# One product in two column parts, and one lower half ahead of an addition, in the feed forward of a hybrid block

## The chip, the cores and the metric

The kernel runs on one core of a Trainium2 chip. The time is the device time of one execution in microseconds (us), the median of several runs. Durations and waits come from one profiled execution, whose times count from the start of its span.

## The reference

The block works on 512 tokens of 1024 features in float32. It joins a convolution branch and a state space branch by gates, multiplies by an output matrix, adds the input, and then applies a gated feed forward of 2816 hidden columns. The change is in the last part:

```python
x = x + rms_norm(mixed, mix_post_g[i])
h = rms_norm(x, ffn_pre_g[i])
gt, up = jnp.split(h @ w_gate_up[i], 2, axis=-1)
f = (jax.nn.silu(gt) * up) @ w_down[i]
x = x + rms_norm(f, ffn_post_g[i])
```

## The kernel before

**Three matmuls for one.** Every large product is taken in a float32r format that TensorE reads. An operand is split in an upper half (a cast, on ScalarE) and a lower half (the value less the upper half, on VectorE, or on ScalarE with an adding DMA from POOL's queue). `mm3` (line 244) issues three matmuls: upper by upper (L246), upper weights by lower moving operand (L248, or L251 twice when it is cut), lower weights by upper moving operand (L252).

**The feed forward in units.** The first product of the feed forward, `h @ w_gate_up`, is made in 22 units `u` of 256 columns, even ones of the gate half and odd ones of the other. A unit is a two by two block product in seven block products of Strassen's kind instead of eight: a11, a12, s2, s1, s3, s4 and a22, by the blocks or sums of blocks of the moving operand (b11, b21, t2, t1, t3, b22, t4). Each has four steps `k` of three matmuls with 256 moving columns: 12 matmuls. `first(u)` issues a11 and a12, `x2` s2, `v1` s1, `x3` s3, `v2` s4, `x4` a22. They add up in PSUM banks that are called xy (parts `X` and `Y`), yv or v in the profile.

**What VectorE and ScalarE do for a unit.** They form the sums of weight blocks (`s1_u` to `s4_u`), the upper halves (`hi_s2_u` and so on, cast into whi_g, chi_g or dhi) and the lower halves (`lo_s2_u`, into wlo_g, clo_g or dlo). They also take results out of PSUM between the products: `begin(u)` copies `X` on ScalarE (`c{u}`) and adds `Y` to it on VectorE (`b{u}`, in line 1396), and only then may `x2` go on adding to the bank.

**Order.** VectorE and ScalarE work in lists written out by hand, `ORDER_DVE` and `ORDER_ACT`: each instruction named there is put behind the one named before it. TensorE's products follow each other in the order in which they are issued.

**Cuts.** `CUT_GU` lists (unit, product, step) for which `mm3` gets `cut=128`: the second of the three matmuls is then issued as two, columns 0 to 127 and 128 to 255 of the same operand and the same output. Two steps of the feed forward have it, and `CUT_PW` names two steps of the convolution's pointwise product in the same way.

Of the kernel before, what the change touches and what calls it, by code (L numbers as in the profile page):

```python
# [59 lines left out]
for _n, _c in PRM:  # L60
# [12 lines left out]
WARM = 7  # L73
CUT = 128
CUT_PW = ((1, "a12", 1), (0, "s3", 1))
CUT_GU = ((0, "a11", 1), (0, "s1", 2))
FIRST = {0: (0, 1), 1: (1, 2), 2: (2, 4), 4: (4, 6), 6: (6, NK)}
LOAD_AT = {0: 0, 1: 1, 2: 2, 3: 4, 5: 6}
RAW_AHEAD = 3
# [11 lines left out]
ADD_S1 = (3, 5)  # L91
ORDER_DVE = (
# [78 lines left out]
def block_kernel(ctx: ExitStack, tc: tile.TileContext, x, xT, x0, prm, hp, gp, wf, w, out):  # L171
# [72 lines left out]
    def mm3(ps, lh, ll, rh, rl, start, stop, more=False, cut=None):  # L244

        mark["pe"] = pe.matmul(ps, lh, rh, start=start, stop=False, skip_group_check=more)  # L246
        if cut is None:
            pe.matmul(ps, lh, rl, start=False, stop=False, skip_group_check=more)  # L248
        else:
            for c in (slice(0, cut), slice(cut, T // 2)):  # L250
                pe.matmul(ps[:, c], lh, rl[:, c], start=False, stop=False, skip_group_check=True)  # L251
        mark["pe3"] = pe.matmul(ps, ll, rh, start=False, stop=stop, skip_group_check=more)  # L252
        return mark["pe"]
# [996 lines left out]
    def product(ps, u, wn, mn, start):  # L1250
# [4 lines left out]
        for k in range(KB):  # L1255
            c = slice(k * P, (k + 1) * P)
            cut = CUT if (u, wn, k) in CUT_GU else None
            m = mm3(ps, wh[:, c], wl[:, c], mh[:, k], ml[:, k], start and k == 0, k == KB - 1, not start, cut)
# [544 lines left out]
```

## Time and profile before

| | us |
|---|---|
| median of 3 runs | 1023.25 (1023.2 to 1023.58) |
| the profiled execution | 1023.47 |
| its span | 1021.7 |
| TensorE, VectorE, ScalarE, GpSimdE busy | 1013.6, 847.3, 617.4, 106.6 |

The feed forward's first product begins at 689.2 us with unit 0 and ends at 908.3 with unit 21, where the down projection begins. A row of a timeline gives the start, the duration, the engine, the line, the operation, and output and inputs by name. The end of a matmul is modelled, so the starts are what to compare. `x2` behind a row means two such instructions in one row.

### The profile page before, as it was taken

How to read it: one execution, taken by the hardware profiler on the slowest of the kernel's cores; microseconds unless marked ns; L12 is line 12 of the kernel's file. 1: busy time of each engine (PE TensorE's matmuls, PEld its weight loads, DVE VectorE, ACT ScalarE, POOL GpSimd, SP SyncE). 2: the span in 40 equal slices, each digit the busy share in tenths (PEclk: the TensorE clock that was granted, in tenths of full speed). 3: DMA queues.
4: the chain of work that ended last, by engine and by line, in shares of the span. 5: the costliest groups of instructions: out<-in, count | busy, mean ns of one | idle time of the engine just before them, and what ended most of it. 6: DMA issues, size and time to landing. Idle time of an engine off the chain costs nothing.

```text
span 1021.7 us, 15941 instructions
## 1 busy us (share of the span) xinstructions
PE 1013.6 (99%) x6183; PEld 888.2 (87%) x6183; DVE 847.3 (83%) x1233; ACT 617.4 (60%) x1038; POOL 106.6 (10%) x138
## 2 busy tenths in 40 slices
PE   9999999999999999999999999999999999999997
PEld 7898889888888888888888899889999999998886
DVE  7899976959595879488987789679998887799974
ACT  7655775666656655663542776476665655568552
POOL 0101101110111012100110110011000000001001
PEclk9999999999999999999999999999999999999999
DMA  8567635645554456446252365635656355459622
GB/s 303 158 168 221 150 89 144 187 130 138 147 163 123 120 170 157 118 138 155 73 145 81 104 199 116 223 100 133 202 152 197 106 146 144 134 168 296 207 83 82
DMA packets 43803, 155.02 MB, mean 152 GB/s; under 512 B 5072, under 2 KB 6096, under 8 KB 42704
## 3 DMA queue, kind: packets, MB, share of 16 engines
q1 hardware_dynamic: 30672, 105.44, 30.2%
q0 software_dynamic: 11136, 43.00, 21.6%
q10 hardware_dynamic: 1920, 5.57, 1.6%
q8 instruction: 48, 0.79, 0.3%
q14 instruction: 27, 0.22, 0.1%
HBM read 149.73 MB, written 4.26 MB: 151 GB/s over the span
## 4 chain that ended last, share of the span: by engine, by line
PE 93%; DVE 3%; ACT 3%; issue 1%; POOL 0%; POOLq 0%; DVEq 0%; ACTq 0%
PE xy L252 4%; PE xy L246 4%; PE xy L248 4%; PE pso L246 3%; PE pso L248 3%; PE pso L252 3%; PE yv L252 3%; PE yv L246 2%; PE yv L248 2%; PE pz L252 2%; PE pz L248 2%; PE pz L246 2%; PE px L252 2%; PE px L246 2%; PE px L248 2%; PE pgs L252 1%
## 5 line engine op out<-in xcount | busy, mean ns | idle before, releaser
L514 DVE SCALAR_TENSOR_TENSOR a<-v,prm_t,a 128x511 f32<-128x511 f32 (+15 forms) x240 | 182.4, 763 | 15.3 <-ACT a L511 13.3
L202 ACT CAST whi<-raw 128x1024 fp32r<-128x1024 f32 x99 | 102.6, 1048 | 128.0 <-PE pso L248 36.6
L209 DVE TENSOR_TENSOR wlo<-raw,whi 128x1024 fp32r<-128x1024 f32 x58 | 70.6, 1219 | 33.0 <-ACT whi L202 32.8
L207 POOL DMA_DIRECT2D wlo<-in_w x41 | 36.5, 891 | 370.6 <-ACT wlo L206 165.0
L248 PE MATMUL pz<-wlo,hhi 128*128 128x512 f32 (+2 forms) x160 | 56.1, 351 | 0.2 <-DVE wlo L209 0.2
L252 PE MATMUL pz<-whi,hlo 128*128 128x512 f32 (+2 forms) x160 | 56.1, 352 | 0.0
L246 PE MATMUL pz<-whi,hhi 128*128 128x512 f32 (+2 forms) x160 | 55.4, 353 | 0.0
L246 PE MATMUL px<-hhi,whi 128*128 128x512 f32 x128 | 50.2, 392 | 0.0
L246 PE MATMUL pso<-yh,whi 128*128 128x512 f32 x128 | 50.2, 394 | 0.0
L252 PE MATMUL px<-hhi,wlo 128*128 128x512 f32 x128 | 49.8, 389 | 0.0
L248 PE MATMUL px<-hlo,whi 128*128 128x512 f32 x128 | 49.8, 389 | 0.0
L248 PE MATMUL pso<-yl,whi 128*128 128x512 f32 x128 | 49.8, 390 | 0.0
L252 PE MATMUL pso<-yh,wlo 128*128 128x512 f32 x128 | 49.7, 389 | 0.0
L1189 ACT CAST whi_g<-raw 128x1024 fp32r<-128x1024 f32 x40 | 41.2, 1051 | 10.6 <-PE yv L248 5.8
L601 DVE SCALAR_TENSOR_TENSOR x<-px,prm_t,x 128x511 f32<-128x511 f32 (+2 forms) x48 | 34.7, 742 | 13.8 <-ACT x L599 13.8
L1196 DVE TENSOR_TENSOR wlo_g<-raw,whi_g 128x1024 fp32r<-128x1024 f32 x34 | 41.3, 1220 | 4.0 <-ACT whi_g L1189 3.7
L206 ACT ACTIVATE wlo<-whi 128x1024 fp32r<-128x1024 f32 x41 | 43.3, 1056 | 0.3
L496 ACT ACTIVATE L<-L,nacs 128x128 f32<-128x128 f32 x128 | 38.8, 389 | 0.5 <-POOL L L489 0.4
L248 PEld LDWEIGHTS pz<-wlo,hhi 128*128 128x128 f32 x160 | 30.2, 188 | 4.5 <-DVE wlo L209 0.6
L246 PEld LDWEIGHTS pz<-whi,hhi 128*128 128x128 f32 x160 | 30.2, 189 | 3.9
L252 PEld LDWEIGHTS pz<-whi,hlo 128*128 128x128 f32 x160 | 30.1, 188 | 3.7
L1189 ACT CAST chi_g<-raw 128x1024 fp32r<-128x1024 f32 x24 | 24.9, 1051 | 7.9 <-PE yv L248 3.8
(761 smaller groups left out, 3459.6 us busy)
## 6 DMA issues: line engine op xcount, KB each, us to landing
raw<-in_w SPq DMA_DIRECT2D x182, 512.0 KB, 4.5
wlo<-in_w POOLq DMA_DIRECT2D x41, 512.0 KB, 6.7
L<-scr POOLq DMA_DIRECT2D x8, 1024.0 KB, 7.9
wlo_g<-in_w POOLq DMA_DIRECT2D x11, 512.0 KB, 7.4
clo_g<-in_w POOLq DMA_DIRECT2D x6, 512.0 KB, 5.5
pws<-in_w POOLq DMA_DIRECT2D x8, 256.0 KB, 5.8
pw_raws<-in_w SPq DMA_DIRECT2D x4, 512.0 KB, 6.3
xr<-in_x ACTq DMA_DIRECT2D x4, 512.0 KB, 4.1
```

The source lines that it names most:

```text
L202: mark[n, c.start] = act.copy(hi[:, c], src)
L206: act.activation(lo[:, c], hi[:, c].bitcast(F32), AF.Copy, scale=-1.0)
L207: mark["lo"] = pool.dma_start(lo[:, c], w[n][:, c].bitcast(F32R), accum_op=ALU.add)
L209: mark["wlo"] = dve.tensor_tensor(out=lo[:, c], in0=src, in1=hi[:, c].bitcast(F32), op=ALU.subtract)
L246: mark["pe"] = pe.matmul(ps, lh, rh, start=start, stop=False, skip_group_check=more)
L248: pe.matmul(ps, lh, rl, start=False, stop=False, skip_group_check=more)
L252: mark["pe3"] = pe.matmul(ps, ll, rh, start=False, stop=stop, skip_group_check=more)
L496: act.activation(L[:, h, c, :], L[:, h, c, :], AF.Exp, bias=nacs[:, c, HG * g + h : HG * g + h + 1])
L514: return dve.scalar_tensor_tensor(out=va[j][:, d:], in0=vs[j][:, : T - d], scalar=col("dw_w", j * KC + KC - 1 - d), in1=va[j][:, d:], op0= ...
L601: dve.scalar_tensor_tensor(out=a[:, d:], in0=ps[:, : T - d], scalar=col("ssm_w", i * KS + KS - 1 - d), in1=a[:, d:], op0=ALU.mult, op1=ALU ...
L1189: a_ = act.copy(hi, src)
L1196: d_ = dve.tensor_tensor(out=lo, in0=src, in1=hi.bitcast(F32), op=ALU.subtract)
```

## The change

The third step of the s2 product of unit 3 (step 2, counted from 0) is cut as well, and VectorE does `lo_s2_3` ahead of the addition `b3`.

```diff
-CUT_GU = ((0, "a11", 1), (0, "s1", 2))
+CUT_GU = ((0, "a11", 1), (0, "s1", 2), (3, "s2", 2))
...
-    "s3_3 x3_1 s2_3 s4_3 lo_s3_2 b3 lo_s2_3 lo_s1_3 x3_2 v2_1 lo_s3_3 g2_1 lo_a11_4 g3_1 g4_1 s1_4 s3_4 s2_4 v2_2 "
+    "s3_3 x3_1 s2_3 s4_3 lo_s3_2 lo_s2_3 b3 lo_s1_3 x3_2 v2_1 lo_s3_3 g2_1 lo_a11_4 g3_1 g4_1 s1_4 s3_4 s2_4 v2_2 "
```

On VectorE, around the addition b3 of unit 3 (xy_6491 is unit 3's bank; wlo_g_6536 is lo_s3_2, wlo_g_6626 is lo_s2_3 and dlo_6630 is lo_s1_3), before:

```order
867 L1196 TENSOR_TENSOR wlo_g_6536<-raw_6267,whi_g_6535 128x1024 [waits Activation_49]
868 L1396 TENSOR_TENSOR f_6544<-xy_6491,f_6544 128x256
869 L1196 TENSOR_TENSOR wlo_g_6626<-raw_6120,whi_g_6625 128x1024 [waits DMASW3_49,DMASW2_49,Activation_49]
870 L1196 TENSOR_TENSOR dlo_6630<-s_3_6619,dhi_6629 128x512
871 L1396 TENSOR_TENSOR sg_1_6698<-xy_6417,sg_1_6698 128x256 [waits PE_49,Activation_49]
```

and now:

```order
867 L1196 TENSOR_TENSOR wlo_g_6536<-raw_6267,whi_g_6535 128x1024 [waits Activation_49]
868 L1196 TENSOR_TENSOR wlo_g_6626<-raw_6120,whi_g_6625 128x1024 [waits DMASW3_49,DMASW2_49,Activation_49]
869 L1396 TENSOR_TENSOR f_6544<-xy_6491,f_6544 128x256
870 L1196 TENSOR_TENSOR dlo_6630<-s_3_6619,dhi_6629 128x512
871 L1396 TENSOR_TENSOR sg_1_6698<-xy_6417,sg_1_6698 128x256 [waits PE_49,Activation_49]
```

The addition and the lower half have changed places, and the rows behind them stand where they stood.

On TensorE, the s2 product of unit 3, before:

```order
3400 L246 MATMUL xy_6491<-t2h,whi_g_6625 128x256 [waits DVE_49,Activation_49]
3401 L248 MATMUL xy_6491<-t2l,whi_g_6625 128x256
3402 L252 MATMUL xy_6491<-t2h,wlo_g_6626 128x256 [waits DVE_49]
3403 L246 MATMUL xy_6491<-t2h,whi_g_6625 128x256
3404 L248 MATMUL xy_6491<-t2l,whi_g_6625 128x256
3405 L252 MATMUL xy_6491<-t2h,wlo_g_6626 128x256
3406 L246 MATMUL xy_6491<-t2h,whi_g_6625 128x256
3407 L248 MATMUL xy_6491<-t2l,whi_g_6625 128x256
3408 L252 MATMUL xy_6491<-t2h,wlo_g_6626 128x256
```

and now:

```order
3400 L246 MATMUL xy_6491<-t2h,whi_g_6625 128x256 [waits DVE_49,Activation_49]
3401 L248 MATMUL xy_6491<-t2l,whi_g_6625 128x256
3402 L252 MATMUL xy_6491<-t2h,wlo_g_6626 128x256
3403 L246 MATMUL xy_6491<-t2h,whi_g_6625 128x256
3404 L248 MATMUL xy_6491<-t2l,whi_g_6625 128x256
3405 L252 MATMUL xy_6491<-t2h,wlo_g_6626 128x256
3406 L246 MATMUL xy_6491<-t2h,whi_g_6625 128x256
3407 L251 MATMUL xy_6491<-t2l,whi_g_6625 128x128 x2
3408 L252 MATMUL xy_6491<-t2h,wlo_g_6626 128x256
```

Row 3407 is two matmuls of 128 columns instead of one of 256. The wait on VectorE in row 3402 is gone; the one in row 3400, on b3, now stands for the lower half too, since b3 comes behind it on VectorE.

## The prediction

> **What bounds the kernel now.** I read the page first, for the engine shares and the chain that ended last; then the busy time by stage; then, since TensorE turned out never to be idle, the start times of its matmuls in the timeline.
>
> ```profile
> PE 1013.6 (99%) x6183; PEld 888.2 (87%) x6183; DVE 847.3 (83%) x1233; ACT 617.4 (60%) x1038; POOL 106.6 (10%) x138
> PE 93%; DVE 3%; ACT 3%; issue 1%; POOL 0%; POOLq 0%; DVEq 0%; ACTq 0%
> ```
>
> TensorE is busy for 99% of the span and is 93% of the chain. So a change pays only if it makes TensorE's stream itself shorter. Busy time can't show that; the distance between the starts of two matmuls can. The changed place is at 720 us, in the first product of the feed forward, whose matmuls have 256 moving columns. Here is TensorE in two stretches (length, busy us, matmuls, granted clock, DMA share, GB/s):
>
> ```profile
> 703.77:718.73 14.96, 14.96 (x135) 1.00 0.53 141
> 721.75:908.31 186.56, 186.56 (x1586) 1.00 0.53 148
> ```
>
> A count includes the two or three matmuls that still ran when the stretch began. Both stretches run from the first matmul of one product to the first of another, and a product has 12: 11 products, 132 matmuls, in the first, and 132 products, 1584 matmuls, in the second. So the spacing is 14.96/132 = 113.3 ns before the place and 186.56/1584 = 117.8 ns after it, at the same granted clock of 1.00, the same width and the same DMA share. The stream has two spacings, 4.45 ns apart, and it changes from the close to the wide one here:
>
> ```profile
> 720.15 0.28 PE L252 MATMUL xy<-t3h,wlo_g 128*128 128x256 f32 x1
> 720.26 0.28 PE L246 MATMUL xy<-t2h,whi_g 128*128 128x256 f32 x1
> 720.37 0.28 PE L248 MATMUL xy<-t2l,whi_g 128*128 128x256 f32 x1
> 720.49 0.37 PE L252 MATMUL xy<-t2h,wlo_g 128*128 128x256 f32 x1
> 720.69 0.28 PE L246 MATMUL xy<-t2h,whi_g 128*128 128x256 f32 x1
> 720.81 0.28 PE L248 MATMUL xy<-t2l,whi_g 128*128 128x256 f32 x1
> ```
>
> The rows are the s2 product of unit 3 (it starts at 720.26). Its third matmul loads the lower half of the weights, wlo_g, and the next starts 0.20 us behind it instead of 0.11. From there on the steps are 0.12. VectorE and ScalarE around it:
>
> ```profile
> 717.85 2.96 ACT L1189 CAST whi_g<-raw 128x1024 fp32r<-128x1024 f32 x3
> 717.73 1.22 DVE L1196 TENSOR_TENSOR wlo_g<-raw,whi_g 128x1024 fp32r<-128x1024 f32 x1
> 718.87 0.42 DVE L1396 TENSOR_TENSOR f<-xy,f 128x256 f32<-128x256 f32 x1
> 719.20 1.22 DVE L1196 TENSOR_TENSOR wlo_g<-raw,whi_g 128x1024 fp32r<-128x1024 f32 x1
> 720.33 0.69 DVE L1196 TENSOR_TENSOR dlo<-s,dhi 128x512 fp32r<-128x512 f32 x1
> ```
>
> The row at 718.87 is the addition b3, the one at 719.20 is lo_s2_3, the half that this product needs. It ends at 720.42; the matmul at 720.49 waited for it, though only by about 0.09 us.
>
> **The change part by part.** *The swap on VectorE.* lo_s2_3 goes ahead of b3. It needs its upper half, the first of ScalarE's three casts from 717.85, done at about 717.85 + 2.96/3 = 718.85; so it can start at about 718.93 in place of 719.20. The addition follows 1.13 us later (719.20 to 720.33 is that step), at 720.06, and ends at 720.48. The product's first matmul waits for b3 in both kernels, because b3 reads the bank that the product goes on adding to. Before, b3 ended at 719.29 and nobody felt it. Now it is what ends last: with the 0.07 us from 720.42 to 720.49 the product starts at about 720.55 instead of 720.26, +0.29 us. The wait at the third matmul goes, since the half is now done before b3: -0.09 us. The lower half behind both (the row at 720.33) keeps its time within 0.1 us, so the products behind see no more delay than that. ScalarE, POOL and SyncE issue the same instructions in the same order. Everything behind the waiting matmul on TensorE moves with it. Net +0.20 us; bounds 0 (the wait only changes its place) and +0.42 (a whole addition).
>
> *The cut.* One matmul of 256 columns becomes two of 128. The trace has four such cuts; the first in the feed forward, at wide spacing, is this one:
>
> ```profile
> 689.29 0.28 PE L248 MATMUL xy<-b11l,a01h 128*128 128x256 f32 x1
> 689.41 0.28 PE L252 MATMUL xy<-b11h,a01l 128*128 128x256 f32 x1
> 689.53 0.28 PE L246 MATMUL xy<-b11h,a01h 128*128 128x256 f32 x1
> 689.65 0.34 PE L251 MATMUL xy<-b11l,a01h 128*128 128x128 f32 x2
> 689.82 0.33 PE L252 MATMUL xy<-b11h,a01l 128*128 128x256 f32 x1
> 689.99 0.28 PE L246 MATMUL xy<-b11h,a01h 128*128 128x256 f32 x1
> ...
> 690.69 0.28 PE L246 MATMUL xy<-b21h,a01h 128*128 128x256 f32 x1
> 690.80 0.28 PE L248 MATMUL xy<-b21l,a01h 128*128 128x256 f32 x1
> ```
>
> From 689.53 to 689.99 it takes 0.46 us where three steps at 0.118 take 0.35: the cut costs +0.11 us. The Trainium skill (TensorE: Matmul & The Clock Gate, section Back-to-back issue gap) states about 81 ns for a matmul of 128 columns in a stream with weight loads, so by that page the cut would cost an estimated 2 x 81 - 113 = 49 ns; the trace's 0.11 us decides. Ahead of the cut the steps are 0.12; at 690.69 they are 0.11. All four cuts, and what follows them:
>
> ```profile
> L251 PE MATMUL pwx<-v_b21l,whi_A x2: 220/248/276, 605.2 to 605.3; 128*128 128x128 f32 x2
> L251 PE MATMUL pwx<-v_t3l,whi_C x2: 221/248/276, 609.5 to 609.5; 128*128 128x128 f32 x2
> L251 PE MATMUL xy<-b11l,a01h x2: 223/250/276, 689.6 to 689.7; 128*128 128x128 f32 x2
> L251 PE MATMUL v<-t1l,dhi x2: 220/248/276, 703.1 to 703.1; 128*128 128x128 f32 x2
> ...
> 610.51:628.08 17.57, 17.57 (x157) 1.00 0.50 133
> 690.69:697.49 6.80, 6.80 (x63) 1.00 0.80 220
> ```
>
> After the second cut 155 matmuls take 17.57 us and after the third 60 take 6.80: both 113.3 ns. After the fourth comes the first stretch quoted, 113.3 ns too. So a cut has left the stream at the close spacing each time, and one of them shows the step from wide to close. The new cut lies 4 matmuls before the end of the product (row 3407 of TensorE's order), so from 721.75 on I expect 113.3 ns: 1584 x 4.45 = 7.05 us less.
>
> *What could take it back.* TensorE comes up to 7 us early at 908, so VectorE must come along. Its busy time by stage:
>
> ```profile
> 720.00:780.00 60.00, 57.42 (x89) 1.00 0.64 185
> 780.00:890.00 110.00, 87.77 (x132) 1.00 0.47 129
> 890.00:908.00 18.00, 17.89 (x28) 1.00 0.52 155
> ```
>
> At the close spacing (113.3/117.8 = 0.962) these stretches become 57.7, 105.8 and 17.3 us. The first holds its 57.42 barely, the second easily, the third misses by 0.6. The operands that come nearest to being late, past the first products:
>
> ```profile
> 729.56 1.23 DVE L1196 TENSOR_TENSOR clo_g<-raw,chi_g 128x1024 fp32r<-128x1024 f32 x1 [0.38 <-ACT chi_g L1189]
> 731.88 0.28 PE L252 MATMUL xy<-t2h,clo_g 128*128 128x256 f32 x1
> 905.76 0.42 DVE L1396 TENSOR_TENSOR f<-xy,f 128x256 f32<-128x256 f32 x1
> 906.90 0.28 PE L246 MATMUL xy<-t4h,whi_g 128*128 128x256 f32 x1
> ```
>
> At 731.88 the margin is 731.88 - 730.79 = 1.09 us. TensorE will have gained (731.88 - 721.75) x 0.038 = 0.38 us by then and lost 0.31 at the start, so it holds. At 906.90 the margin is 0.72 and the third stretch may eat 0.6 of it. A wait there would cost tenths and could turn only the last products wide again. I take nothing for it and put 0.6 us into the range.
>
> *Sum.* -7.05 + 0.11 + 0.20 = -6.74 us. The profiled execution took 1023.47 us (span 1021.7 and 1.77 around it), so 1016.73; the median of the runs is 0.22 lower, so 1016.5. With a little for the last stretch I say 1016.7.
>
> **The rivals.** *The spacing does not come back.* It may be set by what else runs at that time, or the late start of the product may set another one behind the cut. Then only the costs are left: 1023.25 + 0.31 = 1023.6, no change that can be told. For it: nothing in the rows explains why a cut works, and only one cut shows wide ahead and close behind. Against it: four of four. The same page and section of the skill gives one gap for a width, N/2.4 + 2.5 ns, an estimated 109.2 ns at 256 columns, and by it there is nothing to win; the trace has two gaps at one width and one clock, so it does not agree.
>
> *It comes back and is lost again early.* One late operand made it wide at 720.49. If that happens at the tightest place, 731.88, the gain is 0.38 us and the end is 1023.2; if at 780, where VectorE's dense stretch ends, it is 58 x 0.038 = 2.2, less 0.3: 1021.3.
>
> *VectorE can't follow, and TensorE waits product by product.* A late half costs 0.09 us at 720.49. One product earlier the same kind of wait stood, and it cost more:
>
> ```profile
> 718.84 0.28 PE L248 MATMUL xy<-t3l,whi_g 128*128 128x256 f32 x1
> 719.00 0.38 PE L252 MATMUL xy<-t3h,wlo_g 128*128 128x256 f32 x1
> 719.23 0.29 PE L246 MATMUL xy<-t3h,whi_g 128*128 128x256 f32 x1
> ```
>
> Two steps take 0.39 us instead of 0.23, so 0.16 us a wait (and this one left the spacing close: 0.11 by 720.15). Gain and waits balance at 6.74/0.16 = 42 waits in the 132 products; from 55 on the kernel is slower by over 0.2%, and with one in every second product it is 66 x 0.16 = 10.6 us, so 1027.1. For it: 57.42 of 60 us. Against it: 780 to 890 has 22 us to spare, and a stream gone wide by a wait no longer outruns VectorE.
>
> **How the numbers follow.** The runs differ by 0.4 us, and 0.2% is 2.05 us, about what a measurement of this kernel tells from no change. Full gain 0.74 (its own range 1015.8 to 1017.6: 0.2 on the swap, 0.6 on the last stretch, and some tenths for the 512-column stage behind, whose spacing may move either way); lost at about 780 or later 0.08 (1017.6 to 1021.2); never back 0.09; lost before 780 0.03; slower 0.06. The range takes the first two. Faster 0.82, same 0.12, slower 0.06.
>
> **What would show it.** Right: the s2 product of unit 3 starts near 720.55, its third matmul has no wait, the L251 pair is at about 721.4, and from 722 on twelve matmuls take 1.36 us instead of 1.41, up to about 901. Wrong: 0.12 steps behind the pair, or a step of 0.2 us somewhere between 722 and 780 with wide steps after it.

## The result, and the profile after

| | us |
|---|---|
| changed kernel, median of 15 runs | 1017.58 (1016.86 to 1018.43) |
| kernel before, 15 runs of the same comparison | 1023.46 (1016.15 to 1023.91) |
| ratio, 95% interval | 0.9955 (0.9938 to 0.9971) |
| profiled execution of the changed kernel, and its span | 1017.78, 1016.0 |

The changed kernel is faster, by 0.45%. The kernel before has a surprise in it: three of its 15 runs took 1016.15, 1016.43 and 1017.05 us, the other twelve 1023.2 to 1023.91, and none lay between. The same two groups come back in every comparison below: 58 of 108 runs of the kernel before end at 1015.97 to 1018.2, the others at 1022.59 to 1025.25. The granted clock is the same in both, 0.998 to 1.000 in the runs near 1017 and 0.998 to 0.999 in those near 1024. So its median, and every ratio to it, depends on how often each outcome came up (the lower group in 3 of 15, 17 of 35, 24 of 35 and 14 of 23 runs). Where the difference between two kernels matters, I compare the groups themselves.

From the page of the changed kernel, the busy time and the head of the chain:

```profile
PE 1007.7 (99%) x6184; PEld 881.7 (87%) x6184; DVE 847.9 (83%) x1233; ACT 616.9 (61%) x1038; POOL 106.7 (11%) x138
PE 87%; DVE 8%; ACT 3%; issue 1%; DMA 1%; SPq 0%; POOL 0%; POOLq 0%; DVEq 0%; ACTq 0%
```

TensorE has one matmul more and 5.9 us less busy time, at the same 99%: its stream became shorter, and no idle time was filled. TensorE from the product behind the changed place to the end of the stage (length, busy us, matmuls, granted clock, DMA share, GB/s):

```profile
723.05:902.63 179.58, 179.58 (x1586) 1.00 0.54 153
```

These are the 1584 matmuls that took 186.56 us before: 113.4 ns each, 6.98 us less, at the same clock. TensorE's timeline at the place:

```profile
719.84 0.38 PE L252 MATMUL xy<-t3h,wlo_g 128*128 128x256 f32 x1
720.06 0.28 PE L246 MATMUL xy<-t3h,whi_g 128*128 128x256 f32 x1
...
721.00 0.28 PE L252 MATMUL xy<-t3h,wlo_g 128*128 128x256 f32 x1
721.47 0.35 PE L246 MATMUL xy<-t2h,whi_g 128*128 128x256 f32 x1 [0.18 <-DVE f L1396]
721.66 0.28 PE L248 MATMUL xy<-t2l,whi_g 128*128 128x256 f32 x1
721.78 0.28 PE L252 MATMUL xy<-t2h,wlo_g 128*128 128x256 f32 x1
...
722.37 0.33 PE L251 MATMUL xy<-t2l,whi_g 128*128 128x128 f32 x2
722.53 0.33 PE L252 MATMUL xy<-t2h,wlo_g 128*128 128x256 f32 x1
722.71 0.28 PE L246 MATMUL xy<-t2h,whi_g 128*128 128x256 f32 x1
722.82 0.28 PE L248 MATMUL xy<-t2l,whi_g 128*128 128x256 f32 x1
...
723.05 0.28 PE L246 MATMUL v<-t1h,dhi 128*128 128x256 f32 x1
```

The product waits for the addition at its first matmul (721.00 to 721.47) and no longer for the lower half at its third. Eight steps from 720.06 to 721.00 take 0.94 us, so 118 ns: here the wide spacing starts at the wait at 719.84, one product earlier; the same wait stood at 719.00 before and left the stream close. The steps from 721.66 on are 0.12 too. Behind the cut, from 722.71, they are 0.11. VectorE beside it:

```profile
718.56 2.42 DVE L1196 TENSOR_TENSOR wlo_g<-raw,whi_g 128x1024 fp32r<-128x1024 f32 x2
720.90 0.42 DVE L1396 TENSOR_TENSOR f<-xy,f 128x256 f32<-128x256 f32 x1
721.24 0.68 DVE L1196 TENSOR_TENSOR dlo<-s,dhi 128x512 fp32r<-128x512 f32 x1
```

The two lower halves stand together in the first row, and the addition b3 follows at 720.90 and ends at 721.32. The place lies 0.83 us later in this execution than in that of before, and the delay came earlier: the feed forward begins at 690.01 instead of 689.18. From the stage's start to the s3 product that these rows begin with, eleven of the twelve traces agree within 0.02 us (29.54 to 29.56; the one without cuts in the feed forward has 30.21), so I count from the stage's start: v1 of unit 3, the last row, starts 33.04 us behind it, and 32.57 before.

The only other sign of a late operand behind the place is near the stage's end, at the first matmul of unit 21's last product. VectorE's addition ahead of this product, and TensorE:

```profile
900.69 0.42 DVE L1396 TENSOR_TENSOR f<-xy,f 128x256 f32<-128x256 f32 x1
901.10 0.28 PE L252 MATMUL yv<-b22h,wlo_g 128*128 128x256 f32 x1
901.21 0.34 PE L246 MATMUL xy<-t4h,whi_g 128*128 128x256 f32 x1
901.39 0.28 PE L248 MATMUL xy<-t4l,whi_g 128*128 128x256 f32 x1
```

The addition ends at 901.11, 0.10 us ahead of the matmul, and the step from 901.21 is 0.18 instead of 0.11. The profiled executions differ by 1017.78 - 1023.47 = -5.69 us, and +0.83 (ahead of the stage), +0.47 (the place) and -6.98 (the stretch behind it, the small wait in it) make -5.68.

### The profile page after: what moved, and what is told of

Same layout as the page of the kernel before. It is cut to its first block, busy times and chain, and to the rows that moved or that the text cites. A ratio compares the mean times of both kernels' runs of the same rounds, so it can differ in the third digit from the quotient of the medians.

```text
span 1016.0 us, 15943 instructions
## 1 busy us (share of the span) xinstructions
PE 1007.7 (99%) x6184; PEld 881.7 (87%) x6184; DVE 847.9 (83%) x1233; ACT 616.9 (61%) x1038; POOL 106.7 (11%) x138
## 4 chain that ended last, share of the span: by engine, by line
PE 87%; DVE 8%; ACT 3%; issue 1%; DMA 1%; SPq 0%; POOL 0%; POOLq 0%; DVEq 0%; ACTq 0%
PE xy L246 4%; PE xy L252 4%; PE xy L248 4%; PE pso L246 3%; PE pso L248 3%; PE pso L252 3%; PE yv L246 2%; PE yv L252 2%; PE yv L248 2%; PE px L246 2%; PE px L252 2%; PE px L248 2%; DVE a L514 2%; PE pz L248 2%; PE pz L252 2%; PE pz L246 2%
## 6 DMA issues: line engine op xcount, KB each, us to landing
L<-scr POOLq DMA_DIRECT2D x8, 1024.0 KB, 7.6
```

## The experiments

"Close" runs below are those at 1015.8 to 1018.5 us, and "wide" runs those at 1022.5 and above; which spacing a run without a profile had is judged by its time alone. Kernels run together share a chip and the runs of the kernel before.

### The cut alone

```diff
-CUT_GU = ((0, "a11", 1), (0, "s1", 2))
+CUT_GU = ((0, "a11", 1), (0, "s1", 2), (3, "s2", 2))
```

> The kernel before with the cut alone: the addition b3 stays ahead of the lower half. Theory A (the cut sets the close spacing, whatever stands before it; the swap only adds a wait): the wait of 0.09 us at the third matmul of unit 3's s2 product stays, steps of 0.118 us up to the cut, then 113.3 ns per matmul to the end of the stage. 1584 x 4.45 = 7.05 us less, 0.11 for the cut, and none of the about 0.4 us by which that product started late: 1023.4 - 6.9 = 1016.5, and 0.3 to 1.1 below the changed kernel's 1017.6. Theory B (the swap does it, by taking the late half away, and the cut is idle): the stream stays wide, 1023.5.

Measured: 1016.97 us, twelve runs at 1016.5 to 1017.85, against 1023.05 for the kernel before (17 of 35 runs close); ratio 0.9958 (0.9937 to 0.998). Its timeline, with the wait left where it was, and its stage:

```profile
720.67 0.37 PE L252 MATMUL xy<-t2h,wlo_g 128*128 128x256 f32 x1
720.88 0.28 PE L246 MATMUL xy<-t2h,whi_g 128*128 128x256 f32 x1
721.00 0.28 PE L248 MATMUL xy<-t2l,whi_g 128*128 128x256 f32 x1
...
721.35 0.33 PE L251 MATMUL xy<-t2l,whi_g 128*128 128x128 f32 x2
...
722.05 0.28 PE L246 MATMUL v<-t1h,dhi 128*128 128x256 f32 x1
722.16 0.28 PE L248 MATMUL v<-t1l,dhi 128*128 128x256 f32 x1
```

TensorE from there to the stage's end:

```profile
722.04:901.63 179.59, 179.59 (x1586) 1.00 0.56 153
```

Behind the wait at 720.67 the steps up to the cut take 117, 117, 123 and 118 ns, and from 722.05 on they are at 113: this execution is wide ahead of the cut and close behind it. The trace alone doesn't show that the cut did it: in the trace of before, 124 and 118 ns stand behind the wait at 702.27, and 113 follows without a cut. What shows it is the count, twelve close runs of twelve where the kernel before has 17 of 35. The swap isn't needed for it. This is the lowest median of the versions with a new cut: its v1 of unit 3 starts 32.69 us behind the stage's start, so the cut costs 32.69 - 32.57 = 0.12 us and the swap the other 33.04 - 32.69 = 0.35.

### The swap alone

```diff
-    "... lo_s3_2 b3 lo_s2_3 lo_s1_3 ..."
+    "... lo_s3_2 lo_s2_3 b3 lo_s1_3 ..."
```

> The kernel before with the swap alone, no third cut. Theory A: the product waits for b3 at its first matmul (about 0.4 us), and in the changed kernel the steps between that wait and the cut were 0.12; so the stream stays wide to the end of the stage: 1023.5 + 0.4 - 0.1 = 1023.8. Theory B: no half is late any more, so the stream is close from there on: 1023.5 - 7.05 + 0.3 = 1016.8 to 1017.5.

Measured: 1023.91 us, five of twelve runs close (1016.99 to 1017.81), seven wide (1023.81 to 1024.55); ratio 1.0005 (0.9976 to 1.0034). Its profiled execution was a wide one:

```profile
720.30 0.28 PE L252 MATMUL xy<-t3h,wlo_g 128*128 128x256 f32 x1
720.80 0.35 PE L246 MATMUL xy<-t2h,whi_g 128*128 128x256 f32 x1 [0.22 <-DVE f L1396]
720.99 0.28 PE L248 MATMUL xy<-t2l,whi_g 128*128 128x256 f32 x1
```

And its stretch to the stage's end, 117.8 ns a matmul:

```profile
722.28:908.84 186.56, 186.56 (x1586) 1.00 0.53 147
```

A wait for the addition at a product's first matmul can leave the stream wide just as the wait for the lower half did. Its v1 of unit 3 starts 722.28 - 689.33 = 32.95 us behind the stage's start, 0.38 later than in before, so the swap costs 0.35 to 0.38. Neither theory had two outcomes of one kernel; from here on I took a late operand for a toss between two spacings (Theory A2 of the expectations below). The toss is not an even one, nor is its share the same everywhere: 3 of 15 close in one comparison, 24 of 35 in another.

### The cut nine units later

```diff
-CUT_GU = ((0, "a11", 1), (0, "s1", 2))
+CUT_GU = ((0, "a11", 1), (0, "s1", 2), (12, "s2", 2))
```

> The kernel before with the new cut in unit 12's s2 product (about 812 us) instead of unit 3's, no swap. Theory A: a cut works at any place, so the stage is wide from 720 to 812 and close from there to 908: (908.3 - 812.5)/0.1178 = 813 matmuls x 4.45 ns = 3.6 us, less 0.11: 1023.4 - 3.5 = 1019.9. Rival (the two spacings hang on what runs around 720 us, and the cut merely happened there): no change of spacing at 812, 1023.5.

Measured: 1018.37 us; five runs close (1015.81 to 1017.43) and five at 1019.3 to 1021.08, where 1019.9 was expected; ratio 0.9975 (0.9948 to 1.0002). The upper group no longer lies at 1023: a cut in the middle gives back what is left of the stage. The profiled execution was a close one, up to unit 12 with the code of the kernel before:

```profile
720.60 0.28 PE L248 MATMUL xy<-t2l,whi_g 128*128 128x256 f32 x1
720.72 0.37 PE L252 MATMUL xy<-t2h,wlo_g 128*128 128x256 f32 x1
720.92 0.28 PE L246 MATMUL xy<-t2h,whi_g 128*128 128x256 f32 x1
721.04 0.28 PE L248 MATMUL xy<-t2l,whi_g 128*128 128x256 f32 x1
...
721.50 0.28 PE L252 MATMUL xy<-t2h,wlo_g 128*128 128x256 f32 x1
721.62 0.28 PE L246 MATMUL xy<-t2h,whi_g 128*128 128x256 f32 x1
```

TensorE's stretches up to unit 12 and behind its cut:

```profile
721.83:807.90 86.07, 86.07 (x762) 1.00 0.58 166
809.00:901.70 92.70, 92.70 (x819) 1.00 0.51 141
```

The wait is that of before, 0.20 us in place of 0.11. In the trace of before the steps behind it stay at 117 to 119 ns to the end of the product; here they go 120, 117, 116 and then 114 or 113, and the first stretch is 760 matmuls at 113.3 ns. The same code at the same wait, entered at the close spacing in both, fell to the other side. This is the plainest view of the toss.

### A cut in every unit from 3 to 20

```diff
-CUT_GU = (..., (3, "s2", 2))
+CUT_GU = (..., (3, "s2", 2)) + tuple((u, "s2", 2) for u in range(4, 21))
```

The swap is in this one.

> The changed kernel with a cut in every s2 product from unit 4 to 20 as well, 17 more. It measures the price of a cut in a stream that is close already. Theory A: each costs 0.11 to 0.12 us and leaves the stream close: 1017.6 + 17 x 0.115 = 1019.5. Rival (a cut only toggles, or sets the spacing by chance): the stretches between cuts are wide in part, half of them give 3.5 us more: about 1023.

Measured: 1019.84 us (ten runs, 1019.13 to 1020.94). 17 more cuts cost (1019.84 - 1017.58)/17 = 0.13 us each. Two stretches of TensorE in it, the first a whole unit with its cut, the second without one:

```profile
722.96:732.60 9.64, 9.64 (x88) 1.00 0.87 249
732.84:742.25 9.41, 9.41 (x85) 1.00 0.42 138
```

The second is 83 steps of 113.4 ns; the first has 84 matmuls and one more by the cut, and 9.64 - 84 x 0.1134 = 0.11 us is that cut. The spacing was close anyway, so more cuts only cost.

The trace also shows that the toss goes both ways. Ahead of the product of unit 3 the steps are at 117 and 118 ns; it waits for the addition, and from its start at 720.61 the steps are 192, 120, 117, 116, 114, 113 and 114 ns. The stream had come back to the close spacing before the cut.

### No late operand

```diff
-        note(f"s4_{u}", dve.tensor_tensor(...))
+        if u != 3:
+            note(f"s4_{u}", dve.tensor_tensor(...))
```

This kernel leaves out the sum s4 of unit 3's weight blocks, so its values for that unit are others than the reference's; TensorE does the same 6183 matmuls.

> The kernel before without the sum s4_3 on VectorE (0.6 us at 717.1; unit 3's s4 product takes the unsummed block, so its values are others, its work is the same). Both lower halves that TensorE waits for at 719.0 and 720.5 are then done 0.6 us earlier, ahead of their use. No cut in unit 3. Theory A2 (a late operand is a toss: the stream comes out of it close or wide; without a wait it stays as it is): close from 704 to 908 in every execution, 1023.5 - 7.05 - 0.25 = 1016.2, and no times near 1023. Rival (the spacing is tossed anew by something else, such as the DMA traffic of the moment): two groups of times again, near 1016 and 1023.

Measured: 1016.81 us, twelve runs at 1016.01 to 1018.05; the kernel before had 24 of 35 close, median 1017.09; ratio 0.9974 (0.9951 to 0.9996).

```profile
704.80:900.30 195.50, 195.50 (x1727) 1.00 0.55 152
```

No operand is late in unit 3, and the stream stays at 113.3 ns (1725 steps) with neither cut nor swap. So it is the late operand in unit 3 that puts the spacing at risk there, and in this stretch a stream that is close stays close without one.

### A cut at column 64, twice, and at column 192

```diff
-            cut = CUT if (u, wn, k) in CUT_GU else None
+            cut = (64 if u == 3 else CUT) if (u, wn, k) in CUT_GU else None
```

The third kernel has 192 in place of 64. All three have the cut in unit 3 and no swap.

> The cut alone (as in the first experiment), but at column 64: parts of 64 and 192 columns. Theory A2 with any irregular step: the stream is close behind it in every execution, about 1017.0 as with parts of 128. Rival (only two equal parts put weight loads and matmuls back in step): two groups of times, near 1017 and 1023.7.

> The cut at column 64 once more, unchanged. Reading 1 and 2: one to three of twelve near 1023.8, the others near 1017.0. Reading 3: all near 1017.0.

> The cut alone, at column 192: parts of 192 and 64 columns. It tells whether the second part's length matters, after parts of 64 and 192 left the stream wide in 2 of 12 executions and parts of 128 in none of 27. Reading 1 (a part of 64 columns, shorter than the weight load, makes the step irregular, in either order): one to three executions of twelve near 1023.8, the others near 1017.0. Reading 2 (what counts is that the first part is at least 128 columns long): all near 1017.0. Reading 3 (2 of 12 was luck of another kind): all near 1017.0, and also in the repeat of the cut at 64.

Measured at 64: 1017.13 us with 10 of 12 runs close (the kernel before beside it: 24 of 35), then 1023.47 with 4 of 12 close (beside it 14 of 23). Together 14 of 24: no better than the toss, and the eight wide ones of the second twelve are more than any of the readings expected. At 192: 1017.22 us, all twelve at 1016.45 to 1017.52; ratio 0.9971 (0.9948 to 0.9994). That is against Reading 1, which expected some wide runs here too, and fits Reading 2. The timeline of the cut at 192:

```profile
721.19 0.28 PE L246 MATMUL xy<-t2h,whi_g 128*128 128x256 f32 x1
721.30 0.30 PE L251 MATMUL xy<-t2l,whi_g 128*128 128x192 f32 x2
721.44 0.36 PE L252 MATMUL xy<-t2h,wlo_g 128*128 128x256 f32 x1
721.65 0.28 PE L246 MATMUL xy<-t2h,whi_g 128*128 128x256 f32 x1
```

The stretch behind it, at 113.3 ns:

```profile
722.12:901.70 179.58, 179.58 (x1585) 1.00 0.55 153
```

At 128 the pair and the matmul behind it take 0.17 us each, at 192 0.14 and 0.21. The first profiled run at 64 was wide ahead of its cut and close behind it:

```profile
721.46 0.28 PE L246 MATMUL xy<-t2h,whi_g 128*128 128x256 f32 x1
721.58 0.36 PE L251 MATMUL xy<-t2l,whi_g 128*128 128x64 f32 x2
721.78 0.31 PE L252 MATMUL xy<-t2h,wlo_g 128*128 128x256 f32 x1
721.92 0.28 PE L246 MATMUL xy<-t2h,whi_g 128*128 128x256 f32 x1
```

Here a cut with a short first part stands between wide and close steps; by the counts such a cut doesn't turn the stream for sure, and whether it turned this one or the wait ahead did isn't shown. In the second profiled run at 64 the stream was close ahead of the cut already (115, 115 and 113 ns). With a first part of 128 or 192 columns and no later cut in the feed forward, all 51 runs that had one in unit 3 came out close (15 and 12 of the changed kernel, 12 of the cut alone, 12 at 192). The ten runs with 18 cuts can't be counted with them: a spacing lost in unit 3 would have come back at the next cut.

### No cuts in the feed forward

```diff
-CUT_GU = ((0, "a11", 1), (0, "s1", 2))
+CUT_GU = ()
```

> The kernel before without any cut in the feed forward. Theory A2: the stream enters unit 0 wide from the 512-column matmuls (as it does before the cut at 689.6) and stays wide to 697.5, +0.27 us less 0.12 for the missing cut; from there two tosses (at 702 and at 719 to 720.5) in place of one. Times in two or three groups, near 1016.5, 1017.3 and 1024. Rival (the stream comes to the close spacing by itself within some matmuls): 690 to 697 us at 113.3 ns, as before.

Measured: 1024.0 us, 2 of 10 runs close (1017.01, 1017.09); ratio 1.0031 (1.0001 to 1.0061).

TensorE's timeline at the place of the cut that is gone:

```profile
702.38 0.28 PE L246 MATMUL v<-t1h,dhi 128*128 128x256 f32 x1
702.64 0.38 PE L248 MATMUL v<-t1l,dhi 128*128 128x256 f32 x1
702.86 0.28 PE L252 MATMUL v<-t1h,dlo 128*128 128x256 f32 x1
702.98 0.28 PE L246 MATMUL v<-t1h,dhi 128*128 128x256 f32 x1
```

And two stretches behind it:

```profile
703.00:720.00 17.00, 17.00 (x147) 1.00 0.47 124
721.00:812.00 91.00, 91.00 (x775) 1.00 0.57 162
```

Behind the waits at 702.38 and 702.64 the stream is wide: 17.00 us for some 144.5 matmuls (two or three of the 147 ran when the stretch began) is 117.6 ns, and it stays so behind 721. TensorE comes later, and no operand is late at 720, so eight of ten runs kept a wide spacing to the end.

What the cut at 703 does in the kernel before, this run doesn't show, since the cut at 689.6 is gone too. Sixteen matmuls of another kind (`ptr`) stand between units 0 and 1. In the eleven traces with the first cut the stream goes into them close and comes out wide; here it goes in wide and comes out close. The 21 matmuls ahead of the waits at 702, in before and then here:

```profile
699.63:702.10 2.47, 2.47 (x23) 1.00 0.40 159
700.00:702.38 2.38, 2.38 (x24) 1.00 0.27 108
```

That is 117.6 and 113.3 ns. Behind the waits it is the other way round: here 117 and 118 ns, in before 113 and 114 from 702.62 on, ahead of the cut at 703.07. In all eleven traces that have this cut the last step ahead of it takes 113 or 114 ns, so what it is worth isn't shown. In the kernel before TensorE then meets VectorE at 719 to 720, waits there, and may lose the spacing again. The new cut stands behind that wait.

### The changed kernel again

The kernel is the changed one, beside five others on the chip.

> The changed kernel once more, beside the kernel before on this chip. It sizes the swap against the cut alone: Theory A2: 0.4 us above the cut alone (the product starts 0.38 us late, less the 0.09 us wait and plus some tenths of wide steps), so 1017.4, all executions within 1016.8 and 1018.5. Rival (the swap costs nothing, the 0.6 us between the two medians seen so far are other noise): 1017.0.

Measured: 1017.52 us (twelve runs, 1016.85 to 1018.25); ratio 0.998 (0.9959 to 1.0002) to a kernel before that came out close in 24 of 35 runs here. Those 24 have a median of 1016.9, so an execution of before that came out close beats the changed kernel by 0.6 us; one that came out wide (median 1024.07) loses by 6.5.

## Why the prediction was right or wrong

**The spacing, and the 7 us: right.** 1584 steps at 113.4 ns, -6.98 us against the -7.05 of the sum, right up to the stage's end. The rival by which the spacing doesn't come back fell: 113.3 and 117.8 ns stand at one width and one granted clock of 1.00, in executions of the same code. The formula named beside it was not meant for such a stream: the Trainium skill (TensorE: Matmul & The Clock Gate, section Back-to-back issue gap) gives N/2.4 + 2.5 ns as the gap of an isolated matmul, and for a stream with weight loads 81 ns at 128 columns and 131 ns at 512, with no value at 256. By the formula 256 columns would take an estimated 109.2 ns, and the stream shows neither that nor one value alone.

**The cut: right.** 0.11 expected, 0.12 found with the cut alone and 0.13 with 17 more. What the prediction held from four cuts, that the stream is close behind each, held for the new one in every run that can show it. Wide ahead and close behind is plain in the traces of the changed kernel and of the cut at 192. As evidence the four were thinner than they looked: the last of them, at 703, stands in a stream that is close already.

**The swap: the term was too small.** The prediction let the product start 0.29 late and took 0.09 off for the wait, +0.20 in all; the swap cost 0.35 to 0.38. Counted from the stage's start, the product begins 721.47 - 690.01 = 31.46 us in, against 31.08 before: 0.38 late. VectorE did as the prediction had it: with the 0.83 taken off, b3 runs from 720.07 to 720.49, against 720.06 to 720.48. The step that failed is the 0.07 us from VectorE's end to the matmul. That was the distance for a lower half; behind the addition it was 0.15 here (721.32 to 721.47, and 720.65 to 720.80 with the swap alone). And the first step behind this wait is long too, 0.19 instead of 0.11, which eats the 0.09 that was taken off for the old wait. So the wait that the swap was to take away only changed its place. The rest of the swap's 0.55 in the medians (1017.52 against 1016.97, on two chips) is the 0.06 at 901.21 and what the runs scatter.

**What hangs on one wait: right in kind, wrong in certainty.** "One late operand made it wide at 720.49" was read from one execution and taken for the rule. It is one outcome of two, and the traces have both turns: close to wide in before, wide to close with 18 cuts, ahead of the cut. The three runs that I had of the kernel before (1023.2 to 1023.58) all showed the wide one. So the change does not take 7 us off every execution: it takes away the wide outcome, for about 0.5 us on the executions that were close before. Over the 108 runs of the kernel before, with 58 close at about 1017.0 and 50 wide at about 1023.9, the mean is 1020.1, and 1017.5 is 2.6 below it. The median of 15 runs showed most of the 7 us because 12 of them were wide. That share is luck: where 24 of 35 were close, the ratio of the two kernels was 0.998 (0.9959 to 1.0002), no change that can be told.

**What could take it back: right, but for one margin.** No wait stands between 723 and 901. VectorE held, also in its dense stretch up to 780. The margin of 0.72 at 906.90 shrank to 0.10: the matmul at 901.21 is the same one, and TensorE came 5.69 us earlier there, the addition ahead of it only 5.07. That is the 0.6 that the third stretch was to eat, but 0.10 was too little, and the wait cost 0.06. The stream was close behind it. Neither "lost again early" nor "VectorE can't follow" came about.

**The number.** 1016.7 was said and 1017.58 measured. Against the 1016.5 of the sum it is 1.1 us more. Of that, 0.15 is the swap (0.35 for 0.20) and 0.06 the small wait, for which the forecast had added 0.2. Another 0.45 is the base: the twelve wide runs of before in this comparison have a median of 1023.7, where the runs that I started from had 1023.25. The remaining 0.4 is less than the runs scatter.

**Still open.** Why a late operand leaves the stream at one spacing or the other, why it stays there for over a thousand matmuls, and why a cut turns it back, in all 51 runs with a first part of 128 or 192 columns and not in all with 64: the runs show that it does so, not by what.

## What to carry to other kernels

Take the distance between the starts of equal matmuls, stage by stage, where TensorE is never idle: a share of 99% hid 7 us here. Look at all run times before trusting a median: two tight groups are a fork inside the kernel, and a change that settles the fork moves the median by whatever share the groups had. Where a wait is unavoidable, a means to reset the stream pays behind the last risky wait and not ahead of it, once, since each further cut costs 0.13 us.

## What the runs showed of the hardware

- A stream of float32r matmuls of 256 columns runs at 113.3 or 117.8 ns a matmul at full granted clock and keeps the one it has, through 1725 matmuls in one trace (close) and 1584 in others (both).
- An operand that comes 0.1 us late can move it from the close to the wide spacing, or leave it close: 58 of 108 runs of one kernel ended close. A late operand can also move it from wide to close (192, 120, 117, 116, 114, 113 ns behind the wait at 720.61 with 18 cuts), and the spacing changed across sixteen matmuls of another kind too, close to wide in eleven traces and wide to close in one.
- One matmul issued as two, with a first part of 128 or 192 columns, left the stream close in all 51 runs that can show it; with a first part of 64, in 14 of 24, no more than without it. It costs 0.11 to 0.13 us.
